# VectorE in place of GpSimd for the first FFN's first weight tiles, and group norm's reciprocal root by ScalarE and one Newton step

## The chip, the core and the metric

The kernel runs on one core of one Trainium2 chip. A core has five engines that run side by side, each with its own instruction queue, worked through in order: TensorE (PE; its weight loads are listed apart as PEld), VectorE (DVE), ScalarE (ACT), GpSimd (POOL) and SyncE (SP), which here issues the transfers. They synchronise by semaphores. The metric is the time of one execution on the device in microseconds; lower is better.

## The reference

Two layers over a sequence of 512 tokens of 1024 features, in float32. Layer 0 mixes tokens with RWKV-7 (a delta-rule recurrence over 16 heads of 64), layer 1 with a spatial gating unit (SGU). Each is followed by a SwiGLU FFN of width 2816; each sub-layer is wrapped in two RMS norms.

```python
def _rmsnorm(x, g):
    y = x32 * lax.rsqrt(jnp.mean(x32 * x32, axis=-1, keepdims=True) + RMS_EPS)
    return y * g

# end of _rwkv7_time_mix: group norm per head of 64, bonus, gate, output projection
    mu = jnp.mean(y, axis=-1, keepdims=True)
    var = jnp.mean(jnp.square(y - mu), axis=-1, keepdims=True)
    y = (y - mu) * lax.rsqrt(var + GN_EPS)
    y = y * gn_w.reshape(H, N) + gn_b.reshape(H, N)
    y = y + jnp.sum(r_h * k_h * r_k, axis=-1, keepdims=True) * v_h
    return (y.reshape(B, T, D) * g) @ w_o

def _swiglu(x, w_gate, w_up, w_down):
    return (jax.nn.silu(x @ w_gate) * (x @ w_up)) @ w_down

def reference(x, norm_gains, ...):
    for i in range(DEPTH):
        h = _rmsnorm(x, norm_gains[i, 0])
        h = _rwkv7_time_mix(h, ...) if i % 2 == 0 else _sgu_mixer(h, ...)
        x = x + _rmsnorm(h, norm_gains[i, 1])
        h = _swiglu(_rmsnorm(x, norm_gains[i, 2]), ...)
        x = x + _rmsnorm(h, norm_gains[i, 3])
    return x
```

## The kernel before

**Products in three parts.** To keep float32 precision, each large operand is split into a high part (rounded, `whi`, `hT` part 0) and a low part (the rest, `wlo`, `hT` part 1). A product is three matmuls: high by high, high by low, low by high (`mm3`, line 204). The split is two instructions: a copy to the rounded type on ScalarE (line 179) and a subtraction on VectorE (line 180). `weight` (line 182) loads a weight tile of 128x1024 elements into `wraw` by a transfer on SyncE's queue and splits it. With `pool=True` it has its own pair of lines: the copy on ScalarE (line 195) and the subtraction on GpSimd (line 196).

**RWKV (0 to about 450 us).** The heads go in four groups of four (b = 0 to 3). A written plan (`PLAN`) gives the order in which the program states the steps: projections (P), per-group features (E), matrices for chunks of 64 tokens (F, `front`), the triangular inverses (B, `back`: a recurrence of 15 steps on VectorE, lines 910 and 912, on a transposed matrix, then chains of small matmuls with copies into `bdT` between), the scan over chunks (S) and the finish (N). The finish of a group calls `group_norm`, `bonus` and `gated`. `group_norm` takes the mean over 64 (line 1038), subtracts it (1040), squares on ScalarE (1042), sums (1044), calls `rsqrt` on the 16 or 8 sums of each partition, and scales (1046). It runs for groups 0, 1 and 2 over all tokens and for group 3 in two halves of the tokens: five calls, whose roots begin at 287, 334, 396, 420 and 431 us. `gated` transposes on PE (`yt`, 1084), adds the bonus (1085), makes the gate by matmuls (1088) and multiplies (1089); `yt` and `gate` share one bank of PSUM.

**`rsqrt` (line 209).** A reciprocal root wholly on VectorE: scale and offset, a shifted integer guess in two steps, three Newton rounds of three steps: 12 instructions, each needing the one before it. The other routine, `rsqrt1` (line 248), used by the RMS norms, takes ScalarE's root (line 254), VectorE's reciprocal and one Newton step.

**The output projection (`out_proj`, line 273).** It works on two halves of 512 columns, each with four accumulators of 128 tokens. The last weight unit of each half is held back, and the accumulators are then closed token tile by token tile (tt = 0 to 3). `post0` squares half 0 (line 237 on ScalarE) and multiplies it by the gain (line 309 on VectorE), `post1` does the same for half 1 (lines 237 and 317), takes the root (`rsqrt1`) and adds to the residual stream (line 320). The tile `hn` of 1024 columns is scratch: `post1` writes its squares, which nobody reads, into columns 0 to 511 and the scaled half 1 into 512 to 1023. In the RWKV projection (the one called with `spare`), `post0` runs next to `post1` and writes its unread squares into columns 512 to 1023; after tile 0, line 312 computes a root whose result isn't used, so that ScalarE holds the table of the root function from there on. ScalarE has one set of function tables at a time and loads another by an instruction of its own (`ACT_TABLE_LOAD`); copies and squares run under each of the sets seen here. Before line 312 the set is that of the exponential. `norm.step` then transposes the rows of a finished token tile (line 267) and splits them into `hT` (line 60 on ScalarE, line 62 on VectorE).

**The first FFN's first pair.** `plain(0, None)` computes feature tiles j = 0 and 1, each from a gate and an up weight tile. These four tiles are the ones loaded with `pool=True`. Their matmuls go first over tokens 0 to 255, then over 256 to 511, so that they can begin while the last token tiles are still being normed. `Quads` adds up `hT` (line 105) for the later pairs, which use a scheme of seven block products (lines 387 and following). The second FFN receives its first four weight tiles from the SGU (`early`), without `pool`.

**What sets the order.** The program is stated in the order of the code, but the framework that builds it plans the order of each engine's instructions from its own estimates of their times (`schedule_with_timeline_sim=True`), within the data dependences, the banks and buffers, and the few places where the code pins an order. An edit to one instruction can therefore move others, also far behind it.

Of the kernel before, what the change touches and what calls it, by code (L numbers as in the profile page):

```python
# [13 lines left out]
P = 128  # L14
# [116 lines left out]
class Trunk:  # L131
# [77 lines left out]
    def rsqrt(self, ss, n, scale, eps):  # L209
# [13 lines left out]
            v.scalar_tensor_tensor(y, t, 1.5, y, op0=ALU.add, op1=ALU.mult)  # L223
        return y

    def bcast_row(self, row):

        t = self.gp.tile([P, D], F32, name="gain", tag="gain", bufs=2)
        self.nc.gpsimd.dma_start(out=t, in_=row.partition_broadcast(P))
        return t  # L230
# [42 lines left out]
    def out_proj(self, acts, wrows, nk, row, xts, store=None, tail=3, norm=None, spare=None, mid=None, after=()):  # L273


        nc = self.nc
        v = nc.vector
        gain = self.bcast_row(row)
        nu = nk // 2
        cols = [slice(0, 512), slice(512, 1024)]  # L280
        late = (1, 1) if spare else (0, tail)
        accs, f0, part = [None, None], [], []

        def mms(half, k, tt, w):
            tok = slice(tt * P, (tt + 1) * P)
            hi, lo = acts(k)
            self.mm3(accs[half][tt], (hi[:, tok], lo[:, tok]), w, k == 0, k == nk - 1)

        def unit(half, u):
            own = spare if half and u < nu - late[1] else None  # L290
            with ExitStack() as order:
                for ins in after:
                    order.enter_context(self.tc.issue_after(ins.ins))
                hi, lo = self.weight(wrows(u)[:, :, cols[half]], spare=own)
            return [(2 * u + j, (hi[:, j, :], lo[:, j, :])) for j in range(2)]

        def first(half):
            accs[half] = self.accs(half)
            for u in range(nu - late[half]):
                for k, w in unit(half, u):  # L300
                    for tt in range(TT):
                        mms(half, k, tt, w)

        def post0(tt, junk):
            acc = accs[0][tt]
            s = self.sumsq(acc, junk)
            if tt % 2 == 0:
                f0.append(self.f0p.tile([P, 2, 512], F32, name="f0", tag="f0", bufs=2))
            v.tensor_tensor(f0[-1][:, tt % 2, :], acc, gain[:, cols[0]], op=ALU.mult)
            part.append(self.part(s, 1.0 / D, RMS_EPS))  # L310
            if tt == (0 if spare else TT - 1):
                nc.scalar.activation(junk[:, 0:1], part[tt][0], AF.Sqrt)

        def post1(tt, hn):
            acc, lo, hi = accs[1][tt], hn[:, 0:512], hn[:, 512:1024]
            s = self.sumsq(acc, lo)
            v.tensor_tensor(hi, acc, gain[:, cols[1]], op=ALU.mult)
            y = self.rsqrt1(s, part[tt], 1.0 / D)
            for f, c in ((f0[tt // 2][:, tt % 2, :], cols[0]), (hi, cols[1])):
                v.scalar_tensor_tensor(xts[tt][:, c], f, y[:, 0:1], xts[tt][:, c], op0=ALU.mult, op1=ALU.add)  # L320
                if store is not None and tt == TT - 1:
                    nc.sync.dma_start(out=store[tt * P:(tt + 1) * P, c], in_=xts[tt][:, c])
            if store is not None and tt < TT - 1:
                nc.sync.dma_start(out=store[tt * P:(tt + 1) * P, :], in_=xts[tt])

        hn_tile = lambda: self.sm.tile([P, D], F32, name="hn", tag="hn", bufs=2)
        first(0)
        if not spare:
            for tt in range(TT):
                post0(tt, hn_tile()[:, 0:512])  # L330
        if mid:
            mid()
        first(1)
        ends = [[kw for u in range(nu - late[half], nu) for kw in unit(half, u)] for half in range(2)]
        for tt in range(TT):
            for half in range(2):
                for k, w in ends[half]:
                    mms(half, k, tt, w)
            if norm and tt >= LAG:
                norm.step(tt - LAG, xts[tt - LAG])  # L340
            hn = hn_tile()
            if spare:
                post0(tt, hn[:, 512:1024])
            post1(tt, hn)
        if norm:
            for tt in range(TT - LAG, TT):
                norm.step(tt, xts[tt])
            norm.finish()
# [5 lines left out]
    def ffn(self, li, xts, norm, store=None, nxt=None, early=()):  # L354
# [98 lines left out]
        def plain(n, yb):  # L453
            act = self.slot([P, 2, T], F32, "act")
            acts.append(act)
            for f in range(2):
                j = 2 * n + f
                ws = early.pop(0) if early else [self.weight(w[:, :, j * P:(j + 1) * P], pool=j < 2) for w in wgu]
                pp = [self.bank("gu", "gu") for _ in range(2)]
                for c in ((g, u) if j < 2 else (slice(0, 512),)):  # L460
                    for w, ps in zip(ws, pp):
                        for kt in range(KT):
                            self.mm3(ps[:, c], (w[0][:, kt, :], w[1][:, kt, :]), (hT[kt][:, 0, c], hT[kt][:, 1, c]),
                                     kt == 0, kt == KT - 1)
                yb = norm.row() if yb is None else yb
                t = act[:, f]
                v.tensor_tensor(t, pp[0], yb, op=ALU.mult)
                a.activation(t, t, AF.Silu)
                v.tensor_tensor(t, t, pp[1], op=ALU.mult)
                nc.gpsimd.tensor_tensor(t, t, yb, op=ALU.mult)  # L470
            return yb
# [58 lines left out]
    def rwkv(self, x0):  # L530
# [3 lines left out]
        with ExitStack() as ctx:  # L534
# [496 lines left out]
            def group_norm(Y, tts):  # L1031

                n, n4 = len(tts), 4 * len(tts)
                ts = slice(tts[0], tts[-1] + 1)
                y4 = Y[:, ts].rearrange("p t q (h v) -> p (t q h) v", h=2)
                yf = Y[:, ts].rearrange("p t q f -> p (t q f)")
                mu = self.sm.tile([P, n4], F32, name="mu", tag="mu", bufs=2)
                v.tensor_reduce(mu, y4, axis=mybir.AxisListType.X, op=ALU.add)
                v.tensor_scalar(mu, mu, 1.0 / 64, None, op0=ALU.mult)
                v.tensor_tensor(y4, y4, mu.unsqueeze(2).broadcast_to([P, n4, C]), op=ALU.subtract)  # L1040
                sq = self.sm.tile([P, n4, C], F32, name="hn", tag="hn", bufs=2)
                a.activation(sq.rearrange("p q v -> p (q v)"), yf, AF.Square)
                va = self.sm.tile([P, n4], F32, name="va", tag="va", bufs=2)
                v.tensor_reduce(va, sq, axis=mybir.AxisListType.X, op=ALU.add)
                rs = self.rsqrt(va, n4, 1.0 / 64, GN_EPS)
                v.tensor_tensor(y4, y4, rs.unsqueeze(2).broadcast_to([P, n4, C]), op=ALU.mult)

            def bonus(b, o):
# [244 lines left out]
```

## Time and profile before

| | |
|---|---|
| median of 3 runs | 1354.4 us (1348.42 to 1357.36) |
| the profiled execution: time, span | 1345.89 us, 1344.2 us |
| mean granted TensorE clock | 0.979 |
| busy: PE, VectorE, ScalarE, GpSimd | 1279.7, 898.5, 694.9, 166.3 us |
| the four GpSimd subtractions | 461.67, 465.19, 469.19 and 472.66 us, 2.35 to 2.71 us each |
| the unread root of line 312 | 446.64 us: 1.28 us table load, 0.20 us root |

A row of a timeline gives start, duration, engine, line, operation, output<-inputs, shapes and count, and in brackets how long the engine was idle before and what ended that. A row of a table of stretches gives the stretch, its length, the busy time of PE, PEld, DVE, ACT and POOL with instruction counts, then the granted clock of TensorE (1.00 is full speed), the transfer engines' share and GB/s. Idle time of an engine that nobody waits for costs nothing.

### The profile page before, as it was taken

The numbers are of one execution on the slowest core, as the hardware profiler recorded it, in microseconds if no ns is written. First come the engines' busy times: TensorE is split into PE (matmuls) and PEld (weight loads), VectorE is DVE, ScalarE is ACT, GpSimd is POOL, SyncE is SP. The second block draws the span as 40 slices with busy tenths as digits, with TensorE's granted clock in tenths as the row PEclk, the third lists the DMA queues.
The fourth block names the chain that finished last, engine by engine and source line by source line (L and its number), as shares of the span: only waits on it lengthen the run. The fifth ranks groups of instructions, "written<-read, shape, count | busy, mean of one in ns | idle before, by whom it ended". The sixth has DMA issues, their size and how long they took to land.

```text
span 1344.2 us, 24525 instructions
## 1 busy us (share of the span) xinstructions
PE 1279.7 (95%) x9812; PEld 1115.3 (83%) x9812; DVE 898.5 (67%) x1520; ACT 694.9 (52%) x1240; POOL 166.3 (12%) x306
## 2 busy tenths in 40 slices
PE   5999999988989799999999999999999999999997
PEld 3677799887767698899998887878888999998886
DVE  7975846667856589778775325575689878785223
ACT  7976884757443554445454314543464455464221
POOL 0000373665000121000000002020002000000000
PEclk9999999989889999999999999999999999999999
DMA  5146683412143233333323332343430443323231
GB/s 159 47 107 169 165 199 127 123 47 78 45 139 106 72 91 101 107 114 108 106 87 110 94 112 91 93 140 98 142 95 2 125 126 95 97 78 125 94 94 63
DMA packets 217266, 140.10 MB, mean 104 GB/s; under 512 B 67856, under 2 KB 193344, under 8 KB 217152
## 3 DMA queue, kind: packets, MB, share of 16 engines
q1 hardware_dynamic: 215856, 133.81, 34.6%
q0 software_dynamic: 1296, 4.72, 1.0%
q8 instruction: 77, 1.26, 0.4%
q14 instruction: 37, 0.30, 0.1%
HBM read 124.35 MB, written 14.16 MB: 103 GB/s over the span
## 4 chain that ended last, share of the span: by engine, by line
PE 58%; DVE 5%; ACT 1%; issue 1%; DMA 0%; SPq 0%; DVEq 0%; ACTq 0%
PE acc L204 24%; PE Q L204 11%; PE Z L204 7%; PE R L204 7%; PE gu L204 5%; PE u L204 3%; DVE wlo L180 1%; DVE wsum L387 1%; PE s L1227 1%; PE ptr L267 0%; ACT whi L179 0%; DVE braw L106 0%; DVE hT L62 0%; DVE bc L180 0%; DVE x L320 0%
## 5 line engine op out<-in xcount | busy, mean ns | idle before, releaser
L180 DVE TENSOR_TENSOR wlo<-wraw,whi 128x1024 fp32r<-128x1024 f32 x109 | 133.6, 1226 | 197.8 <-ACT whi L179 197.4
L179 ACT CAST whi<-wraw 128x1024 fp32r<-128x1024 f32 x109 | 114.2, 1048 | 224.1 <-PE acc L204 140.9
L204 PE MATMUL acc<-whi,actw 128*128 128x512 f32 x704 | 220.7, 394 | 0.0
L204 PE MATMUL Q<-bc,whi 128*128 128x256 f32 x864 | 157.2, 282 | 3.5 <-ACT hn L431 2.2
L204 PEld LDWEIGHTS acc<-whi,actw 128*128 128x128 f32 x704 | 132.3, 188 | 30.7
L204 PE MATMUL acc<-wlo,actw 128*128 128x512 f32 x352 | 138.7, 394 | 0.0
L204 PEld LDWEIGHTS Q<-bc,whi 128*128 128x128 f32 x864 | 133.8, 190 | 4.3 <-ACT hn L431 2.6
L179 ACT CAST whi<-wsum 128x1024 fp32r<-128x1024 f32 x72 | 75.2, 1050 | 90.3 <-PE Q L204 31.3
L204 PE MATMUL Q<-bc,wlo 128*128 128x256 f32 x432 | 121.7, 282 | 0.0
L204 PE MATMUL Z<-bc,whi 128*128 128x256 f32 x576 | 106.8, 283 | 0.0
L204 PE MATMUL R<-bc,whi 128*128 128x256 f32 x576 | 105.3, 281 | 0.8 <-ACT whi L179 0.8
L180 DVE TENSOR_TENSOR wlo<-wsum,whi 128x1024 fp32r<-128x1024 f32 x72 | 87.0, 1220 | 20.3 <-ACT whi L179 19.1
L204 PE MATMUL gu<-hT,whi 128*128 128x256 f32 (+1 forms) x384 | 91.5, 331 | 5.0 <-DVE hT L62 3.6
L179 ACT CAST whi<-wq 128x1024 fp32r<-128x1024 f32 x54 | 56.6, 1049 | 66.0 <-PE R L204 22.3
L204 PEld LDWEIGHTS R<-bc,whi 128*128 128x128 f32 x576 | 88.9, 188 | 1.3 <-ACT whi L179 1.0
L204 PEld LDWEIGHTS Z<-bc,whi 128*128 128x128 f32 x576 | 89.7, 190 | 0.1
L180 DVE TENSOR_TENSOR wlo<-wq,whi 128x1024 fp32r<-128x1024 f32 x54 | 67.4, 1250 | 28.8 <-ACT whi L179 28.7
L204 PE MATMUL Z<-bc,wlo 128*128 128x256 f32 x288 | 81.4, 283 | 2.3 <-DVE wlo L180 2.3
L204 PE MATMUL proj<-xsp,whi 128*128 128x512 f32 x256 | 82.4, 401 | 1.3 <-ACT r L674 1.3
L204 PEld LDWEIGHTS Q<-bc,wlo 128*128 128x128 f32 x432 | 82.1, 190 | 0.0
L204 PE MATMUL R<-bc,wlo 128*128 128x256 f32 x288 | 81.0, 281 | 0.0
L204 PEld LDWEIGHTS acc<-wlo,actw 128*128 128x128 f32 x352 | 66.0, 188 | 15.3
(346 smaller groups left out, 2841.2 us busy)
## 6 DMA issues: line engine op xcount, KB each, us to landing
wraw<-in_ffn_w_down_dram SPq DMA_DIRECT2D x44, 512.0 KB, 3.7
wq<-in_ffn_w_gate_dram SPq DMA_DIRECT2D x72, 256.0 KB
wq<-in_ffn_w_up_dram SPq DMA_DIRECT2D x72, 256.0 KB, 4.2
wraw<-in_rwkv_w_rkv_dram SPq DMA_DIRECT2D x24, 512.0 KB, 5.4
wraw<-in_sgu_w_in_dram SPq DMA_DIRECT2D x16, 512.0 KB, 4.5
x<-in_x_dram SPq DMA_DIRECT2D x8, 512.0 KB, 3.4
ST<-sb SPq DMA_DIRECT2D x8, 512.0 KB
MV<-sa SPq DMA_DIRECT2D x32, 128.0 KB, 3.5
```

Source lines behind the costliest of these rows:

```text
L179: self.nc.scalar.copy(hi, src)
L180: self.nc.vector.tensor_tensor(lo, src, hi.bitcast(F32), op=ALU.subtract)
L204: self.nc.tensor.matmul(out, l, r, start=start, stop=stop, skip_group_check=resumed)
L387: v.tensor_tensor(s, x, y, op=ALU.add)
L1227: mm(acc[:, tt * P:(tt + 1) * P], vt[tt][:, m * P:(m + 1) * P], wsT[:, m, :], start=True, stop=True)
```

## The change

Group norm's reciprocal root is computed by a new routine, `rsqrtn`: scale and offset on VectorE, the root on ScalarE, the reciprocal and one Newton step of three instructions on VectorE. The unread root at line 312 is left out where the projection is the RWKV one (it stays in the others). In that projection `post0` writes its unread squares into columns 0 to 511. The first FFN's first four weight tiles are split like all others, the subtraction on VectorE.

```diff
+    def rsqrtn(self, ss, n, scale, eps):
+        sm, v = self.sm, self.nc.vector
+        c, r, m = (sm.tile([P, n], F32, name=t, tag=t) for t in ("nr_a", "nr_y", "nr_t"))
+        v.tensor_scalar(c, ss, scale, eps, op0=ALU.mult, op1=ALU.add)
+        self.nc.scalar.activation(r, c, AF.Sqrt)
+        v.reciprocal(r, r)
+        v.tensor_tensor(m, r, r, op=ALU.mult)
+        v.scalar_tensor_tensor(m, m, -0.5, c, op0=ALU.mult, op1=ALU.mult)
+        v.scalar_tensor_tensor(r, m, 1.5, r, op0=ALU.add, op1=ALU.mult)
+        return r
...
             part.append(self.part(s, 1.0 / D, RMS_EPS))
-            if tt == (0 if spare else TT - 1):
+            if not spare and tt == TT - 1:
                 nc.scalar.activation(junk[:, 0:1], part[tt][0], AF.Sqrt)
...
             if spare:
-                post0(tt, hn[:, 512:1024])
+                post0(tt, hn[:, 0:512])
             post1(tt, hn)
...
-                ws = early.pop(0) if early else [self.weight(w[:, :, j * P:(j + 1) * P], pool=j < 2) for w in wgu]
+                ws = early.pop(0) if early else [self.weight(w[:, :, j * P:(j + 1) * P]) for w in wgu]
...
-                rs = self.rsqrt(va, n4, 1.0 / 64, GN_EPS)
+                rs = self.rsqrtn(va, n4, 1.0 / 64, GN_EPS)
```

## The prediction

> **What bounds the kernel now.** I read the page first, then the chain of waits, then tables of equal stretches, and last the timeline of each engine around the edited lines. The page:
>
> ```profile
> span 1344.2 us, 24525 instructions
> PE 1279.7 (95%) x9812; PEld 1115.3 (83%) x9812; DVE 898.5 (67%) x1520; ACT 694.9 (52%) x1240; POOL 166.3 (12%) x306
> PE 58%; DVE 5%; ACT 1%; issue 1%; DMA 0%; SPq 0%; DVEq 0%; ACTq 0%
> ```
>
> PE is busy for 95% of the span and heads the chain that ended last. Its own work is not edited, so a gain can come from two places only: the 64.5 us (1344.2 - 1279.7) in which PE waits, and stretches in which it runs at a reduced clock. The edits lie between the first group norm (287 us) and the first FFN pair (about 476 us). The table of stretches (columns: stretch, its length, busy time of PE, weight load, VectorE = DVE, ScalarE = ACT, GpSimd = POOL, then the granted clock, DMA share, GB/s) shows where PE loses there:
>
> ```profile
> 328.00:338.00 10.00, 6.91 (x190) 6.01 (x186) 9.83 (x31) 5.17 (x9) 3.69 (x8) 0.67 0.31 106
> 338.00:348.00 10.00, 7.93 (x89) 6.61 (x88) 9.47 (x25) 3.22 (x6) 0.00 (x0) 0.50 0.01 2
> 283.61:287.02 3.41, 1.53 (x14) 1.40 (x13) 3.33 (x4) 2.99 (x8) 2.24 (x5) 0.99 0.23 79
> 287.02:290.44 3.42, 3.42 (x17) 3.20 (x16) 3.01 (x14) 2.87 (x7) 1.76 (x4) 0.51 0.03 5
> 386.01:389.42 3.41, 1.95 (x13) 1.27 (x10) 1.43 (x3) 1.62 (x2) 0.00 (x0) 1.00 0.11 28
> 389.42:392.84 3.42, 2.67 (x23) 2.28 (x25) 2.62 (x4) 1.47 (x4) 0.00 (x0) 1.00 0.60 171
> 447.45:450.86 3.41, 1.25 (x8) 0.94 (x7) 2.11 (x8) 3.05 (x11) 0.00 (x0) 0.99 0.10 29
> 450.86:454.28 3.42, 3.42 (x11) 2.65 (x10) 3.04 (x11) 0.25 (x1) 0.00 (x0) 0.51 0.56 152
> 464.51:467.93 3.42, 0.80 (x5) 0.35 (x3) 3.35 (x7) 3.42 (x13) 2.35 (x1) 0.99 0.53 153
> 467.93:471.34 3.41, 1.36 (x6) 1.36 (x7) 3.41 (x12) 2.83 (x8) 2.15 (x1) 0.50 0.52 154
> ```
>
> I chose these 3.41 us stretches because the clock changes on that grid. After a stretch in which PE was busy for 1.25 or 1.53 us the next runs at about half clock; after one with 1.95 us it runs at full clock. So a wait costs its own length, and, where it takes PE below somewhere between 1.53 and 1.95 us of 3.41 (45% to 57%), up to 1.7 us more (3.42 x (1 - 0.51)).
>
> **Part A, the root in group norm (five calls).** The old routine issues 12 VectorE instructions a call, the new one 5 and a ScalarE root: 35 fewer on VectorE, 5 more on ScalarE. One of the root's groups by line from 276 to 460 us (busy us, mean ns), then VectorE's timeline in the first call, in the second, and after the third and the last:
>
> ```profile
> L222 DVE SCALAR_TENSOR_TENSOR nr_t<-nr_t,nr_a 128x16 f32<-128x16 f32 (+1 forms) x15 | 2.6, 176 | 0.3
> 283.63 1.22 DVE L1044 TENSOR_REDUCE va<-hn 128x16 f32<-128x1024 f32 x1 [2.48 <-ACT hn L1042]
> 287.25 0.38 DVE L214 TENSOR_SCALAR nr_a<-va 128x16 f32<-128x16 f32 x1
> 290.15 0.17 DVE L223 SCALAR_TENSOR_TENSOR nr_y<-nr_t,nr_y 128x16 f32<-128x16 f32 x1
> 335.75 0.28 DVE L912 TENSOR_TENSOR Dm<-Dm,tm 128x110 f32<-128x110 f32 x1
> 335.94 0.17 DVE L222 SCALAR_TENSOR_TENSOR nr_t<-nr_t,nr_a 128x16 f32<-128x16 f32 x1
> 336.06 0.28 DVE L910 TENSOR_TENSOR tm<-LX,Dm 128x120 f32<-128x120 f32 x1
> 342.13 0.28 DVE L912 TENSOR_TENSOR Dm<-Dm,tm 128x120 f32<-128x120 f32 x1
> 342.45 0.27 DVE L910 TENSOR_TENSOR tm<-LX,Dm 128x110 f32<-128x110 f32 x1
> 414.89 0.69 DVE L1089 TENSOR_TENSOR ob<-gate,ob 128x512 f32<-128x512 f32 x1 [5.66 <-PE gate L1088]
> 439.99 0.42 DVE L1089 TENSOR_TENSOR ob<-gate,ob 128x256 f32<-128x256 f32 x1 [3.30 <-PE gate L1088]
> ```
>
> 35 x 0.176 us is 6.2 us of VectorE time. Little of it is on PE's path. First call: PE is busy all through 287.02 to 290.44. Second call, where VectorE is full: the triangular recurrence (L910, L912) steps from 335.75 to 336.06 with a root step between, 0.31 us, and from 342.13 to 342.45 without one, 0.32 us, so the root steps fill gaps and their removal returns almost nothing. After the third and the last call VectorE stands idle for 5.66 and 3.30 us until PE has made the gate. If nevertheless all reached PE, the first call would give 7 of the 12 steps of its 3.07 us (290.32 - 287.25), less the trip to ScalarE of about 0.4: 1.4 us, and the second some 0.6, so -2.0 is the lower end.
>
> Against that stand a new wait and a table load. VectorE takes its instructions in order: its reciprocal waits for the root, and behind it wait the bdT copies, the recurrence and the MV sums, for which PE waits. The row at 283.63 shows the price of such a wait in this very routine: VectorE stood 2.48 us for ScalarE's square. The first root also needs its table (1.28 us) and itself (0.29; both rows stand in part B) on a ScalarE that is busy for 2.99 of 3.41 us there; its copies behind would be 1.6 us late. Upper end: 2.5 + 1.6 = +4.1. No row shows this root in this place; between the ends I take 0, nearest to the recurrence's rows, because the order of instructions is planned anew with the root in it and has other work to put between.
>
> The Trainium skill (ScalarE: Activation LUTs, "What ACT_TABLE_LOAD costs") charges about 1.38 us of drain beside the 1.28 us load, 2.66 us in all. The rows of part B have the next instruction directly behind the load. By the page, A's upper end would be +5.5, and B's removal below would be worth 1.38 us more.
>
> **Part B, the end of the output projection (L312, and the scratch half).** Since the group norm leaves the root's table loaded, the early root at L312 goes. ScalarE's timeline, VectorE's, PE's:
>
> ```profile
> 446.64 1.28 ACT L312 ACT_TABLE_LOAD   x1 [0.86 <-DVE rh L245]
> 447.93 0.20 ACT L312 ACTIVATE hn<-rc 128x1 f32<-128x1 f32 x1
> 448.04 0.58 ACT L237 ACTIVATE hn<-acc 128x512 f32<-128x512 f32 x1
> 449.18 0.29 ACT L254 ACTIVATE rr<-ss,rc 128x1 f32<-128x1 f32 x1
> 448.75 0.69 DVE L317 TENSOR_TENSOR hn<-acc,gain 128x512 f32<-128x512 f32 x1 [2.12 <-ACT hn L237]
> 450.26 0.40 DVE L1089 TENSOR_TENSOR ob<-gate,ob 128x256 f32<-128x256 f32 x1
> 448.27 0.28 PE L1088 MATMUL gate<-sgb,g2x 96*128 96x256 f32 x1
> 450.72 0.64 PE L1084 MATMUL yt<-ident,Y 128*128 128x128 f32 x2 [2.16 <-DVE ob L1089]
> ```
>
> This is a chain: load and root on ScalarE, then the square at 448.04, then L317, for which VectorE idled 2.12 us, then L1089, then PE's transpose after 2.16 us. The gate was done at 448.55, so L1089 could come 1.7 us earlier at most; the square can come 1.4 us earlier (448.04 - 446.64). I take 1.2. That lifts PE's busy time in 447.45:450.86 from 1.25 to about 2.4 of 3.41 us, above the 1.95 that kept full clock, so the next stretch gains up to 1.7 us; I take 1.5, for VectorE must keep up. B = -2.7, ends -3.1 and 0 (the next accumulator, not this load, may be what the square would wait for). Nothing is added here, so B has no end above 0. Moving the scratch to the other half costs nothing: L317 still waits for the square of the accumulator it reads. Once this stall is gone, the next late thing is the start of the FFN, part C.
>
> The Trainium skill (TensorE: Matmul & The Clock Gate, "HAM oscillation") asks only for no idle gap over about 3.4 us. The wait of 2.16 us in front of a half-clock stretch speaks against it; by the page the sum would lose the 1.5.
>
> **Part C, the four wlo tiles.** GpSimd's timeline, VectorE's, PE's, and the page's price of the same operation on VectorE:
>
> ```profile
> 465.19 2.35 POOL L196 TENSOR_TENSOR wlo<-wraw,whi 128x1024 fp32r<-128x1024 f32 x1 [1.13 <-ACT whi L195]
> 472.66 2.44 POOL L196 TENSOR_TENSOR wlo<-wraw,whi 128x1024 fp32r<-128x1024 f32 x1 [0.76 <-ACT whi L195]
> 463.06 0.69 DVE L309 TENSOR_TENSOR f<-acc,gain 128x512 f32<-128x512 f32 x1 [3.55 <-ACT hn L237]
> 465.54 2.02 DVE L257 SCALAR_TENSOR_TENSOR rt<-rr,rm 128x1 f32<-128x1 f32 x1
> 471.73 3.99 DVE L105 TENSOR_TENSOR braw<-hT 128x256 f32<-128x256 f32 x5
> 484.32 1.09 DVE L105 TENSOR_TENSOR braw<-hT 128x256 f32<-128x256 f32 x3
> 469.98 0.58 PE L204 MATMUL gu<-hT,whi 128*128 128x256 f32 x1 [3.29 <-DVE hT L62]
> ```
>
> A subtraction on VectorE takes 1.22 us, as the group has it:
>
> ```profile
> L180 DVE TENSOR_TENSOR wlo<-wraw,whi 128x1024 fp32r<-128x1024 f32 x109 | 133.6, 1226 | 197.8 <-ACT whi L179 197.4
> ```
>
> Added: 4 x 1.22 = 4.9 us on VectorE. Returned: the 128x1 step at 465.54 took 2.02 us and ended as GpSimd's tile did (467.54), against 0.17 for such small steps: 1.8; the five L105 at 471.73 took 0.80 each beside GpSimd, the three at 484.32 without it 0.36: 2.2. Net +0.9. The first tile fits into the 3.55 us idle before 463.06. On the path to hT, whose late half PE awaited for 3.29 us, 1.8 goes and one tile (1.2) may come: -0.6. The third and fourth tiles lie before the hT of the last tokens: 2.4 - 2.2 = +0.2. C = -0.4. Clock: both stretches from 464.51 to 471.34 lie far below the threshold (0.80, 1.36) and 0.6 us more won't lift the first; I take 0. Ends: -3.5 (1.8 and a half-clock stretch of 1.7) and +3.2 (two tiles ahead of hT, 2.4 - 1.8 = 0.6, 0.9 later, and a stretch of 1.7).
>
> **Sum.** 0 - 2.7 - 0.4 = -3.1 us. The profiled execution took 1345.9 us (its span of 1344.2 and 1.7 around it), so it becomes 1342.8. The three runs before have a median of 1354.4, 8.5 above the profiled one; against them the forecast is 1351.3, given as 1351.
>
> **Rivals** (times against the median).
> 1. All of it counts: A -2.0, B -3.1, C -3.5: -8.6, 1346. For it: VectorE is full from 328 to 348 us, where PE has its longest half-clock stretch. Against: the recurrence's unchanged step.
> 2. Slower: VectorE stands at the reciprocal, in its first call and again in the second. It decides once the root comes later than the 1.4 us that the missing steps save. Price: 4.1 + 1.7 for a half-clock stretch, then 2.5 + 1.7: +10.0; with B and C +6.9: 1361. For it: the 2.48 us at 283.63. Against: the planned order has other work for the gap.
> 3. VectorE becomes the bound at the FFN's start: C +3.2 eats B: +0.5, 1355. For it: VectorE busy 3.35 and 3.41 of 3.41 us.
> 4. No clock comes back, since another wait takes the place of the one in B within the same stretch: -1.6, 1353. It is also what the Trainium skill's clock rule (TensorE: Matmul & The Clock Gate, "HAM oscillation") would give.
> 5. The new plan shuffles the work from 287 us on with results that no row prices: up to 15 either way.
>
> **Numbers.** Chances: forecast 0.35; rivals 0.22, 0.13, 0.11, 0.11, 0.08. Runs of the same kernel differ by 9 us (1348.4 to 1357.4), so about 1%, 13.5 us, is what can be told from no change. Each case carries about 4.5 us to either side for that. Forecast and rivals 1, 3 and 4 span 1341 to 1360; with rival 2 mostly below that end, 1340 to 1360 leaves out less than 2 in 10. Faster by over 1% (under 1341) takes the low tail of rival 1 and half of rival 5: 0.12. Slower by over 1% (over 1368) takes the tails of rivals 2 and 5: 0.05. Within 1%: 0.83.
>
> **What would show it.** A: 25 VectorE steps under the new routine, a table load in front of the first root and none in the projection; wrong if VectorE's idle time before the reciprocal exceeds 1.4 us with PE waiting then. B: no load at 446 us, PE's wait for L1089 at about 1 us, no half-clock stretch behind it. C: no small VectorE step of 2 us; PE's wait for hT under 3 us. The prediction is wrong if PE's waits before 287 us or after 490 us change, or if PE's summed waits move by over 6 us.

## The result and the profile after

The changed kernel took 1338.3 us (median of 4 runs, 1334.5 to 1340.7) against 1351.4 for the kernel before in the same series (4 runs): a ratio of 0.990 with a 95% interval of 0.987 to 0.993. Another series gave 1338.0 against 1349.4, 0.992 (0.990 to 0.994). The forecast was 1351, a gain of 3.1, with a range of 1340 to 1360; the gain is 11 to 13 us, and the time lies 2 us below the range.

Lines of the kernel after that lie behind line 225 stand 12 higher than before (L949, the copies into `bdT`, is L961; L910 and L912, the recurrence, are L922 and L924). From the page of the kernel after:

```profile
span 1339.0 us, 24501 instructions
...
PE 1278.9 (96%) x9812; PEld 1114.0 (83%) x9812; DVE 892.5 (67%) x1489; ACT 694.8 (52%) x1244; POOL 160.7 (12%) x302
```

PE waits for 60.1 us of the span (1339.0 - 1278.9), 4.4 less than before. The two profiled spans differ by 5.2 us only: the profiled run of before lies 5.5 us under the median of its series (1345.9 against 1351.4), that of after 2.5 above its own (1340.7 against 1338.3), which together makes the 13.1 us between the medians.

**Where the time went.** I took the same events in both traces and compared the distance between them. The largest change lies around group norm's second call. VectorE's timeline, first before, then after, at the two ends of that stretch:

```profile
266.97 1.99 DVE L916 STREAM_TRANSPOSE Dt<-Dm 128x1024 f32<-128x1024 f32 x1
367.27 0.68 DVE L935 TENSOR_TENSOR Qs<-Qp,id 128x512 f32<-128x512 f32 x1
```

```profile
270.62 1.95 DVE L928 STREAM_TRANSPOSE Dt<-Dm 128x1024 f32<-128x1024 f32 x1
363.24 0.68 DVE L947 TENSOR_TENSOR Qs<-Qp,id 128x512 f32<-128x512 f32 x1
```

The stretch took 100.3 us before and 92.6 after: -7.7. As rows of a table of stretches, before and after:

```profile
266.97:367.27 100.30, 88.78 (x1615) 76.59 (x1615) 73.91 (x174) 57.87 (x138) 39.98 (x92) 0.88 0.19 54
```

```profile
270.62:363.24 92.62, 83.71 (x1615) 72.39 (x1615) 70.98 (x160) 59.34 (x141) 39.85 (x92) 0.94 0.22 59
```

PE's idle time fell from 11.5 us (100.30 - 88.78) to 8.9, and the same 1615 matmuls kept it busy for 5.1 us less, at a mean clock of 0.94 in place of 0.88. So about two thirds of the gain is busy time that went by at a higher clock. What differs in the stretch is the planned order, and in it first of all where the copies into `bdT` of the group before stand in VectorE's queue. Before and after, in the order of time, with the last and first steps around them:

```profile
327.40 1.97 DVE L896 STREAM_TRANSPOSE LX<-LA 128x1024 f32<-128x1024 f32 x1
...
336.26 0.17 DVE L223 SCALAR_TENSOR_TENSOR nr_y<-nr_t,nr_y 128x16 f32<-128x16 f32 x1
336.35 0.67 DVE L949 COPY bdT<-Tp 32x512 f32<-32x512 f32 x1
...
337.97 0.69 DVE L949 COPY bdT<-Tp 32x512 f32<-32x512 f32 x1
...
343.92 0.69 DVE L968 COPY bdT<-T2p 32x512 f32<-32x512 f32 x1
```

```profile
328.18 1.95 DVE L908 STREAM_TRANSPOSE LX<-LA 128x1024 f32<-128x1024 f32 x1 [0.53 <-POOL LA L845]
330.05 0.64 DVE L961 COPY bdT<-Tp 32x512 f32<-32x512 f32 x1
...
332.29 0.69 DVE L961 COPY bdT<-Tp 32x512 f32<-32x512 f32 x1
...
338.94 0.24 DVE L232 RECIPROCAL nr_y<-nr_y 128x16 f32<-128x16 f32 x1
...
341.44 0.69 DVE L980 COPY bdT<-T2p 32x512 f32<-32x512 f32 x1
```

Before, the first copy started 8.95 us after the start of the `LX` transpose, behind group norm's mean, square sum and the first Newton round. After, it starts 1.87 us after it, ahead of all of them. PE needs these copies for its next products (`mp`). PE's waits from 318 to 368 us, before and after (line that waited, who released it, us in total, times, longest):

```profile
PE mvt L923 <- ACT MVt L926: 3.1, 1, 3.1
PE mp L973 <- DVE bdT L968: 1.9, 1, 1.9
```

```profile
PE Q2p L967 <- issue: 0.8, 1, 0.8
PE Yp L1034 <- ACT su L1026: 0.8, 1, 0.8
```

The waits of 3.1 and 1.9 us are gone. They hang on two queues. The one of 1.9 us is for a `bdT` copy on VectorE, the one of 3.1 us for a copy into `MVt` on ScalarE. ScalarE's timeline, before and after:

```profile
331.36 1.06 ACT L1042 ACTIVATE hn<-Y 128x1024 f32<-128x1024 f32 x1 [1.84 <-issue]
332.44 1.07 ACT L926 COPY MVt<-mvt 128x512 f32<-128x512 f32 x2
```

```profile
335.02 1.06 ACT L1054 ACTIVATE hn<-Y 128x1024 f32<-128x1024 f32 x1
```

Before, ScalarE idled 1.84 us in front of group norm's square, with the `MVt` copies behind it. The square reads what VectorE's subtraction of the mean (L1040) writes, which was done at 331.01 us; the profile names no engine for this wait, so its cause is read from the order and the code. After, the mean and the subtraction stand behind the first `bdT` copy, and ScalarE has other copies to do until the square can start: it doesn't idle there.

The two stretches quoted in the prediction, 328 to 338 and 338 to 348 us, read so after (columns as there):

```profile
328.00:338.00 10.00, 7.86 (x205) 6.32 (x204) 9.63 (x17) 7.84 (x18) 5.85 (x13) 0.91 0.39 122
338.00:348.00 10.00, 9.71 (x84) 8.81 (x82) 9.56 (x32) 3.64 (x6) 0.00 (x0) 0.75 0.01 2
```

PE went from 6.91 and 7.93 us busy at clock 0.67 and 0.50 to 7.86 and 9.71 at 0.91 and 0.75. VectorE is as full as before. So it isn't VectorE's load that has changed, but the order in which it and ScalarE work.

**The other steps in the trace after.** The first call on ScalarE and VectorE; the projection end on ScalarE and PE, with its stretches; the FFN's start on VectorE and PE:

```profile
288.79 1.28 ACT L231 ACT_TABLE_LOAD   x1
291.04 0.22 ACT L231 ACTIVATE nr_y<-nr_a 128x16 f32<-128x16 f32 x1 [0.97 <-DVE nr_a L230]
...
445.45 0.29 ACT L266 ACTIVATE rr<-ss,rc 128x1 f32<-128x1 f32 x1
445.63 0.59 ACT L249 ACTIVATE hn<-acc 128x512 f32<-128x512 f32 x1
```

```profile
291.29 0.25 DVE L232 RECIPROCAL nr_y<-nr_y 128x16 f32<-128x16 f32 x1 [0.28 <-ACT nr_y L231]
...
461.00 1.21 DVE L180 TENSOR_TENSOR wlo<-wraw,whi 128x1024 fp32r<-128x1024 f32 x1
```

```profile
445.49 0.44 PE L1096 MATMUL yt<-ident,Y 128*128 128x128 f32 x2 [0.79 <-DVE ob L1101]
446.66 0.50 PE L204 MATMUL acc<-whi,oT 128*128 128x512 f32 x1 [0.73 <-ACT oT L179]
...
463.85 0.58 PE L204 MATMUL gu<-hT,whi 128*128 128x256 f32 x1 [1.13 <-DVE hT L62]
```

```profile
445.33:448.75 3.42, 2.52 (x13) 2.02 (x14) 3.25 (x13) 1.57 (x7) 0.00 (x0) 1.00 0.51 153
448.75:452.16 3.41, 3.41 (x16) 2.62 (x15) 3.33 (x9) 0.41 (x1) 0.00 (x0) 1.00 0.02 7
```

The table load lies in front of the first root and none in the projection. VectorE stood 0.28 us at the reciprocal. PE's wait for the gate's product at the projection end fell from 2.16 to 0.79 us (with 0.73 behind it), and the stretches from there on run at full clock in this trace.

### The profile page after: what moved, and what is told of

Same layout as the page of the kernel before. It is cut to its first block, busy times and chain, and to the rows that moved or that the text cites. A ratio compares the mean times of both kernels' runs of the same rounds, so it can differ in the third digit from the quotient of the medians.

```text
span 1339.0 us, 24501 instructions
## 1 busy us (share of the span) xinstructions
PE 1278.9 (96%) x9812; PEld 1114.0 (83%) x9812; DVE 892.5 (67%) x1489; ACT 694.8 (52%) x1244; POOL 160.7 (12%) x302
## 4 chain that ended last, share of the span: by engine, by line
PE 62%; DVE 10%; DMA 3%; ACT 2%; issue 2%; SPq 1%; POOL 1%; DVEq 0%; ACTq 0%; POOLq 0%
PE acc L204 27%; PE Q L204 10%; PE Z L204 7%; PE R L204 7%; PE gu L204 5%; PE u L204 3%; DVE wlo L180 2%; DMA wq<-in_ffn_w_up_dram 1%; DVE wsum L399 1%; PE gh L992 1%; DMA wraw<-in_rwkv_w_o_dram 1%; DVE hT L62 1%; PE s L1239 1%; ACT whi L179 0%; DVE bc L180 0%
## 5 line engine op out<-in xcount | busy, mean ns | idle before, releaser
L180 DVE TENSOR_TENSOR wlo<-wraw,whi 128x1024 fp32r<-128x1024 f32 x113 | 139.6, 1235 | 194.3 <-ACT whi L179 193.7
L179 ACT CAST whi<-wraw 128x1024 fp32r<-128x1024 f32 x113 | 118.4, 1049 | 232.0 <-PE acc L204 146.0
```

Source lines behind the costliest of these rows:

```text
L179: self.nc.scalar.copy(hi, src)
L180: self.nc.vector.tensor_tensor(lo, src, hi.bitcast(F32), op=ALU.subtract)
```

## The experiments

Parts as in the prediction: A is the root in group norm, B the projection end (early root and scratch half), C the four `wlo` tiles. At first there were two theories of A's gain. *Order*: the planned order of the second call, with `bdT` early, makes it. *Steps*: the fewer VectorE steps make it.

### Each part alone

A alone puts `rsqrtn` into the kernel before; B alone has the two edits of the projection; C alone has the edit of the weight tiles.

> Part A alone on the kernel before: the new root in group norm; the early root at the projection, its scratch half and the GpSimd tiles stay. Three theories. Steps: the 35 missing VectorE instructions (6.2 us) count, -5 to -7 us. Order: the new root matters because the plan of the stretch from 326 to 350 us comes out with the bdT copies ahead of group norm's mean, where before they stood behind it and PE waited 3.1 and 1.9 us and ran at half clock; -6 to -8 us, all of it won between 325 and 350 us, about +1.6 lost at the first call to the table load. The prediction's: steps hidden, 0, at most -1.3 because the load at the projection is gone too.

> Part B alone: the early root at the projection is left out and the scratch half moved, old root, GpSimd tiles. The load of the root's table is then still needed for the projection's first real root. All theories: the square comes 1.4 us earlier but the load now stands before the first root, behind which no PE work waits at once: -1 to 0 us; the half-clock stretch behind 450 us may go (-1.7 more). If B itself is worth the 2.7 us of the prediction without A, PE's wait for L1101 (L1089 before) falls from 2.2 to about 1 us.

> Part C alone: the four subtractions on VectorE, all else as before. The prediction's: -0.4 us (-3.5 to +3.2), no 128x1 step of 2 us on VectorE, PE's wait for hT 3.3 -> 2.7. Order theory: about -2.5, since from 400 to 575 us the changed kernel won 5.1 us of which B is 2.7. If C is worth nothing, the drift against before stays at 0 through 575 us.

Measured beside 1351.2 us for the kernel before: A 1345.3, ratio 0.9957 (0.9938 to 0.9975); B 1350.7, 0.9998 (0.9976 to 1.0019); C 1348.3, 0.9978 (0.9956 to 1.0001). A gains 5.9 us, all others little: most of the gain was not where the forecast had it. A's time lies in the range of both theories, so it doesn't tell them apart. B alone can't save the load. ScalarE's and PE's timeline of B alone:

```profile
460.94 1.28 ACT L266 ACT_TABLE_LOAD   x1
```

```profile
463.10 0.44 PE L1096 MATMUL yt<-ident,Y 128*128 128x128 f32 x2 [1.90 <-DVE ob L1101]
```

Without A, the load only moves to the projection's first used root, and PE still waits 1.90 us. B alone also leaves the order of all instructions as it was.

### More or fewer steps, and an order forced by hand

Group norm keeps the old root, with one, two or four Newton rounds in place of three:

```diff
-                rs = self.rsqrt(va, n4, 1.0 / 64, GN_EPS)
+                rs = self.rsqrt(va, n4, 1.0 / 64, GN_EPS, 1)    # 2, 4
```

> The kernel before with one Newton round instead of three in group norm's root: 6 VectorE steps a call, no ScalarE root, no table load (the root is accurate to some 0.2% only, two rounds of its refinement are left out). Steps theory: 6 steps x 5 calls x 0.17 = -5.2 us. Order theory: the planned order from 326 us has the bdT copies right behind the transpose, as in the changed kernel, so -5 to -8, between 325 and 350 us. If the ScalarE root itself brought the gain: 0.

> The kernel before with two Newton rounds instead of three: 9 steps a call (one round of refinement left out). Steps theory: -2.6 us. Order theory: the bdT copies stand in the middle, behind the mean and half of the recurrence but ahead of the root: between 0 and -4, not in proportion to the steps.

> The kernel before with four Newton rounds instead of three: 15 steps a call. Steps theory: +2.6 us. Order theory: the bdT copies stand behind the root as before, so 0 to +1.5; the order after that stretch differs, which can be worth some us either way.

Two kernels keep the old root and pin the order of the second call: one holds the mean behind the first `bdT` copy, the other holds the mean and four recurrence steps each behind one of the copies.

```diff
-                v.tensor_reduce(mu, y4, axis=mybir.AxisListType.X, op=ALU.add)
+                with tc.issue_after(late.ins) if late else ExitStack(): v.tensor_reduce(mu, y4, axis=mybir.AxisListType.X, op=ALU.add)
```

> The kernel before, old 12-step root and all, with one more order: the mean of the second group norm call (from 326 us) may not be issued on VectorE before the first bdT copy of group 2's inverse. Only that stretch's order changes. Order theory: most of part A's gain comes without any step saved, -4 to -8 us between 325 and 350 us, and PE's wait for MVt of 3.1 us is gone. Steps theory and the prediction's: 0 within 2 us.

> The kernel before, old 12-step root, with the order of the stretch from 326 us forced: on VectorE the first bdT copy of group 2 goes ahead of the mean of group 1's norm and of step 0 of group 3's recurrence, the second ahead of step 1, the Q2 copy ahead of step 3, the copy from T2p ahead of step 6 (the first attempt held back only the mean, and the plan put the copies behind the recurrence). Order theory: no step is saved, yet -4 to -8 us appear between 325 and 350 us, and PE's waits for MVt (3.1) and for the bdT copy from T2p (1.9) shrink. Steps theory and the prediction's: 0 in that stretch; behind it the plan may differ.

Measured: one round 1348.4, 0.9977 (0.9958 to 0.9997); two rounds 1364.4, 1.0084 (1.0054 to 1.0114); four rounds 1361.6, 1.0074 (1.0047 to 1.010); the mean held 1353.6, 1.0007 (0.998 to 1.003); all held 1360.6, 1.0068 (1.004 to 1.010). The steps theory falls: with two rounds VectorE has 15 steps fewer than before and the kernel is 12 us slower. The times that the order theory gave were missed as well: it had -5 to -8, 0 to -4 and 0 to +1.5 us for one, two and four rounds, and the runs gave -4.0, +12.0 and +9.3. In the stretch itself it came closer (-7.0, -1.5 and +2.3 in the table of all runs below); the rest is what the plan changed further on.

The two pinned kernels missed too: neither gained. With the mean held, the plan moved the copies still further back, behind 11 of the 15 steps of the recurrence. PE's wait for `MVt` shrank from 3.1 to 0.3 us, as expected, but its wait for `bdT` grew from 1.9 to 4.3: the two waits do hang on two queues. With all held, the copies are early in the queue, but VectorE stands in front of the first until PE has made what it copies; that copy, the stretch and the waits of that kernel:

```profile
334.32 0.68 DVE L961 COPY bdT<-Tp 32x512 f32<-32x512 f32 x1 [4.18 <-PE Tp L956]
```

```profile
328.00:338.00 10.00, 7.84 (x278) 6.51 (x278) 4.88 (x7) 6.15 (x15) 4.76 (x13) 0.91 0.40 122
```

```profile
PE mp L985 <- DVE bdT L980: 2.2, 1, 2.2
PE us L1021 <- DVE MV L994: 2.1, 1, 2.1
```

VectorE is busy for 4.88 us of 10 where it had 9.83. So an early place in the queue alone is not shown to gain anything. What gains is the whole order that the plan makes when it puts the copies early of itself.

### Order and steps taken apart

Which root the *first* call has decides the planned order of the *second*: in the kernels built here the copies come early with 5 or 6 VectorE steps in the first call's root, in the middle with 9, and late with 12 or 15. So the whole change was split by call: once the second call alone keeps the old root (its 12 steps, but `bdT` early), once the first call alone does (the second call has the 5 steps, but `bdT` late).

```diff
-                rs = self.rsqrtn(va, n4, 1.0 / 64, GN_EPS)
+                rs = (self.rsqrtn if self.__dict__.setdefault('gnc', []).append(1) or len(self.gnc) in (1, 3, 4, 5) else self.rsqrt)(va, n4, 1.0 / 64, GN_EPS)    # mirror: (2, 3, 4, 5)
```

> The changed kernel once more, beside the next three, so that they can be compared with it on one chip. Both theories: 1338 us, between 1334 and 1341, ratio 0.990 to the kernel before.

> The whole change, but the second group norm call (the one beside the recurrence) keeps the old root with its 12 VectorE steps. The plan still puts the bdT copies right behind the LX transpose: that order is set by the first call's root. Order theory (the gain of part A comes from the place of the bdT copies): as the changed kernel, 1338 to 1342 us; in the stretch from 346 to 367 us it still gains 7 us or more on the kernel before; the seven more steps cost 7 x 0.176 = 1.2 us at the most. Steps theory (fewer VectorE steps in the stretch where VectorE is full): most of part A's 5.9 us is gone, 1344 us or more.

> The mirror of the run before: the whole change, but the first group norm call keeps the old root; the second and the later ones have the new one. The plan now puts the bdT copies of the second call late, behind the whole new root. Order theory: part A's gain is gone, 1343 to 1349 us, with PE's waits for the bdT copies or MVt of 3 us or more between 318 and 368 us and no gain over the kernel before between 346 and 367 us. Steps theory: the second call has its five steps, so the gain stays: 1337 to 1341 us.

> Parts A and B without C (the four wlo tiles stay on GpSimd). Alone, A measured 1345.3 (-5.9 us), B 1350.7 (-0.5), C 1348.3 (-2.9): together -9.3, while the whole change gave -13.1. If B is worth its 2.7 us only where A leaves the table loaded, ab gives -5.9 - 2.7 = -8.6, about 1342.7 us, and C adds its 2.9 and a little more. If instead the surplus comes from C beside A, ab is at 1345 (as A alone).

Measured beside 1349.4: the changed kernel 1338.0; old root in the second call 1341.6, 0.9938 (0.992 to 0.996); old root in the first call 1359.8, 1.0081 (1.005 to 1.011); A and B without C 1337.8, 0.9907 (0.989 to 0.993). The old steps with the early order keep 7.8 of the 11.4 us, the new steps with the late order lose everything and 10 us more. The first is inside the range of the order theory. The mirror is slower than either theory had it, and A and B are faster than both forecasts for them. VectorE's timeline of the mirror, and PE's, here and further on in the projection:

```profile
327.96 1.96 DVE L908 STREAM_TRANSPOSE LX<-LA 128x1024 f32<-128x1024 f32 x1
335.79 0.25 DVE L232 RECIPROCAL nr_y<-nr_y 128x16 f32<-128x16 f32 x1
337.05 0.67 DVE L961 COPY bdT<-Tp 32x512 f32<-32x512 f32 x1
```

```profile
PE mvt L935 <- ACT MVt L938: 3.1, 1, 3.1
```

```profile
433.59 0.66 PE L1071 MATMUL vt<-ident,hn 128*128 128x128 f32 x4 [1.29 <-ACT ob L1073]
435.03 0.69 PE L1096 MATMUL yt<-ident,Y 128*128 128x128 f32 x2 [0.78 <-ACT ob L1073]
```

The wait of 3.1 us is that of the kernel before. The second place, at 433 us, is one reason why the mirror is slower than before, not just equal (+9.2 us in the second stretch of the table below; a weight sum in the second layer comes with 6.3 more in the third). Its plan puts PE's transposes `vt` of the last group's bonus behind the projection's first products, PE waits 1.29 and 0.78 us, and clock 0.50 follows from 435 to 440 us.

### What B adds beside A

A, B and C alone add up to -9.3; A and B together gave -11.6. Yet the trace of A alone has no load at the projection end, and PE's wait there is 0.79 us already. These runs were made side by side: A alone; A without the early root; A and B; and the whole change with the new root in the first call only.

```diff
-            if tt == (0 if spare else TT - 1):          # A without the early root: this edit alone
+            if not spare and tt == TT - 1:
```

> Part A alone once more, beside the next three. Its trace has no table load at the projection end (the group norm leaves the table in place) and PE's wait for L1101 there is 0.8 us, not 2.16. Theory of order: most of the whole gain is here, -8 to -10 us, about 1341 us; the -5.9 of the first call was low by the spread of the two calls (each ratio carries +-0.002, 2.7 us). Theory of an own gain of B: -5 to -6 us again, about 1345 us.

> Part A and the early root of the projection removed; the scratch half as before. Theory of order: within 1 us of part A alone (the root that goes is 0.2 us without a load). Theory that the early root matters: as A with both edits.

> Parts A and B, without C, once more: 1338 us. Theory of order: within 3 us of part A alone. Theory that the scratch half is what gains (the second half's product no longer waits for the square that writes the same half): 4 to 6 us below part A and below A with the early root removed.

> The whole change, with the new root in the first group norm call only; the four later calls keep the old root and its 12 VectorE steps. The plan puts the bdT copies of the second call early, as in the changed kernel. Theory of order: 1339 to 1343 us, as the run with the old root in the second call alone (1341.6). If the new root itself is worth its steps in the later calls: 1346 us or more.

Measured beside 1350.1: A 1343.6, 0.9950 (0.993 to 0.997); A without the early root 1343.9, 0.9942 (0.992 to 0.996); A and B 1336.2, 0.9879 (0.985 to 0.991); new root in the first call only 1340.0, 0.9914 (0.988 to 0.994). The early root brings nothing that shows (0.3 us); the scratch half, which was thought to cost and bring nothing, comes with some 7 us. The first call's root alone brings nearly the whole gain of the change. Its own steps can't be what brings it: that root took 3.07 us before and takes 1.42 in the trace after (290.85 to 292.27 us). The 7 us are not at the projection (second stretch of the table below). PE's timeline, then VectorE's, of A alone, in the second layer, 600 us behind the edit:

```profile
1043.11 0.58 PE L204 MATMUL Z<-bc,whi 128*128 128x256 f32 x1 [2.98 <-DVE bc L180]
```

```profile
1039.56 1.23 DVE L399 TENSOR_TENSOR wsum<-wq 128x1024 f32<-128x1024 f32 x1 [2.63 <-DMA wq<-in_ffn_w_up_dram]
1040.70 1.22 DVE L399 TENSOR_TENSOR wsum<-wsum,wq 128x1024 f32<-128x1024 f32 x1
1041.84 1.22 DVE L180 TENSOR_TENSOR bc<-tsum,bc 128x1024 fp32r<-128x1024 f32 x1
```

The same place of A and B, VectorE:

```profile
1038.39 1.22 DVE L399 TENSOR_TENSOR wsum<-wsum,wq 128x1024 f32<-128x1024 f32 x1
1039.53 1.22 DVE L180 TENSOR_TENSOR bc<-tsum,bc 128x1024 fp32r<-128x1024 f32 x1
1040.66 2.35 DVE L399 TENSOR_TENSOR wsum<-wq 128x1024 f32<-128x1024 f32 x2
```

In A alone the plan put one weight sum, `wsum<-wq`, ahead of `bc`, and VectorE stood 2.63 us for its transfer with `bc` behind it. PE waited 2.98 us, and its clock was 0.66 on average from 1040 to 1050 us. In A and B that sum stands behind `bc`, and PE doesn't wait.

Two more runs have the scratch half without that order (A and the half, early root kept; two sums ahead of `bc`) and that order without the half (A and C):

> Part A and the scratch half; the early root of the projection stays. In its plan the second layer's bc (L180, at about 1040 us) stands behind two sums (L399) that wait for their DMA, one more than in A alone. Theory of the plan: PE waits 3 us or more for bc there and the run is as slow as A alone or slower, 1343 to 1348 us, although it has the scratch half. Theory that the half as such gains: 1336 to 1339 us, as A with both of B's edits.

> Parts A and C without B (scratch half and early root as before). In its plan the second layer's bc stands ahead of both sums, as in the changed kernel. Theory of the plan: no wait for bc, 1336 to 1341 us, as the changed kernel, without any of B's edits. Theory that the half as such gains: 1343 to 1345 us, as A alone.

Measured beside 1350.9: A and the half 1344.4, 0.9938 (0.991 to 0.996); A and C 1342.9, 0.9943 (0.992 to 0.996). The first has the time that the theory of the plan gave, with the half and as slow as A alone, but not the wait: PE doesn't stand for `bc`. It waits 4.7 us for `hT` at the start of the first FFN and 2.5 us at 1060.7 us for a `wlo`, ahead of which VectorE stood 3.03 us for the transfer of two more sums. The second missed: PE has no wait for `bc`, but the run is no faster than A alone. It loses at the start of the first FFN, where PE waits 1.69 and 1.20 us. So the place of `bc` is not all that B brings beside A; the plan of the first FFN is a further part. From the fourth `x<-hn,ry,x` of line 332 to the third `wsum<-wsum,wq` (478.3 to 543.9 us before) A and C took 2.6 us more than the kernel before, the change 1.2 and 1.4 less (two traces): some 4 us lie there.

### All runs together

The distance between the same events in each trace, less that of the kernel before. *First*: from the second `Dt` transpose to the fourth `Qs` sum, the stretch of 100.3 us above. *Second*: from the mean of the fifth group norm call to the second `x<-hn,ry,x` of line 332 (426.0 to 455.7 before, 29.7 us). *Third*: from the tenth such step to the 36th `wsum<-wsum,wq` (976.1 to 1196.5 before, 220.4 us).

| kernel | ratio | `bdT` copies | sums ahead of `bc` | first | second | third |
|---|---|---|---|---|---|---|
| after | 0.990 | early | 0 | -7.7 | -0.2 | +1.8 |
| after, again | 0.992 | early | 0 | -8.3 | -0.2 | +1.8 |
| A and B | 0.991 | early | 0 | -9.5 | -0.2 | +1.6 |
| A and B, again | 0.988 | early | 0 | -8.3 | +0.7 | +1.4 |
| new root in call 1 only | 0.991 | early | 0 | -6.5 | +5.0 | +1.0 |
| old root in call 2 only | 0.994 | early | 0 | -7.7 | +2.7 | +2.2 |
| A and C | 0.994 | early | 0 | -8.4 | -0.7 | +1.5 |
| one Newton round | 0.998 | early | 0 | -7.0 | +4.9 | +2.1 |
| A | 0.996 | early | 1 | -7.2 | -0.7 | +7.2 |
| A, again | 0.995 | early | 1 | -7.5 | -0.7 | +5.0 |
| A without the early root | 0.994 | early | 1 | -8.7 | -0.6 | +6.4 |
| A and the half | 0.994 | early | 2 | -7.5 | +0.1 | +5.3 |
| C | 0.998 | late | 0 | +0.9 | 0.0 | +0.7 |
| B (order of before) | 1.000 | late | 0 | +7.7 | -0.5 | +1.9 |
| mean held | 1.001 | later | 0 | +5.2 | -0.4 | +0.1 |
| all held | 1.007 | early, forced | 0 | +4.4 | +0.8 | +0.8 |
| old root in call 1 only | 1.008 | late | 1 | +0.7 | +9.2 | +6.3 |
| four Newton rounds | 1.007 | late | 1 | +2.3 | +4.9 | +4.7 |
| two Newton rounds | 1.008 | in the middle | 2 | -1.5 | +10.1 | +8.5 |

Each is one profiled run, and B, whose order is that of before, is off by 7.7 us in the first stretch (clock 0.66 from 340 to 350 us), so a single figure there says little. The groups say more: every kernel whose plan puts the copies early of itself gains 6.5 to 9.5 us in the first stretch, no other over 1.5; and every kernel with a sum ahead of `bc` loses 4.7 to 8.5 in the third, no other over 2.2. In the 12 kernels of the first group PE idles for 7.2 to 9.7 us of the first stretch and has 6.8 to 17.1 us at half clock; in the other seven and in the kernel before it is 10.5 to 14.6 and 13.7 to 34.1.

## Why the prediction was wrong

**The bound** was read right: PE, its waits and its clock, between 287 and 490 us. The largest loss was even quoted, the stretches at 328 and 338 us. It was not asked what PE waited for there (`MVt` 3.1 us, `bdT` 1.9 us) and what stood in VectorE's and ScalarE's queues ahead of that; only the price of the root's own steps was. The rule for the clock, half after 1.53 us busy and full after 1.95, doesn't hold even in the trace it was read from: PE was busy for 2.09 us from 273.32 to 276.73 and for 2.07 from 327.93 to 331.34, and half clock followed both.

**Part A**: the step that failed is "between the ends I take 0 ... because the order of instructions is planned anew with the root in it and has other work to put between". That the root's steps fill gaps agrees with the runs: with the new root in the first call only (28 VectorE steps more than the change) the kernel is at 0.991, as the change. The new wait stayed small too: 0.28 us in the first call, against a limit of 1.4, so rival 2 doesn't occur there. (No row showed the trip of about 0.4 us to ScalarE in the lower end; these 0.28 us are what VectorE stood for it.) But a new plan was taken as something that cushions, not as something that shifts. A alone measured -5.9 and -6.5 us, outside its lower end of -2.0. In its two traces the first stretch is 7.2 and 7.5 us shorter: the new order around the second call took away PE's waits of 3.1 and 1.9 us and part of the half-clock time, and for that no term of the sum stood. The same plan put a weight sum ahead of `bc` in the second layer, and the third stretch lost 7.2 and 5.0 us, against 1.0 to 2.2 in the early kernels without one. Whether A would be faster by the difference isn't shown, for A and C, which has no such sum, isn't.

**Part B**: most of the mechanism was right: no load, and the wait down from 2.16 to 0.79 us (about 1 was forecast). The 1.5 us for the clock were not secured: the same waits of 0.79 and 0.73 us were followed by full clock in the trace after and by half clock in that of A and B, again (last section). Two more things were wrong. It comes with A, as A alone has it; and its -2.7 was too large: from the mean of the fifth call to the copy `hn<-yb` at 492.0 us A alone, A again and A without the early root took 65.0, 64.5 and 64.4 us, 66.0 before, so 1.0 to 1.6 less, and PE's own progress (the 100th matmul `gu<-hT,whi`, also 66.0 before) was 66.3, 65.8 and 65.8, almost as before. "Moving the scratch to the other half costs nothing" holds of the instruction (B alone: 0.9998), not of the plan: beside A and without the early root it came with 7 us, in part through the place of `bc`.

**Part C**: as told, no 2 us step of one column, and PE's waits for `hT` in front of the FFN's products fell from 1.4 and 3.3 us to 0.9 and 1.4, though its transposes now wait 1.7 us for `hT`, which they did not before. The 0.80 us of each of the five L105 steps was the mean of a merged row: one took 2.60 us, the others 0.41, so GpSimd's tile held up one step. The 2.2 us come out the same, and in C alone all 12 such steps take 0.40 to 0.42. -0.4 was forecast; alone it gave -2.9 (-5.9 to +0.1), beside A and B nothing (1338.0 with it, 1337.8 without). The size is inside the ends given, and stays unclear.

**The rivals.** Rival 5, "the new plan shuffles the work from 287 us on with results that no row prices: up to 15 either way", is what happened, in both directions: from 0.988 to 1.008 among kernels whose own instructions differ by a few us. It had a chance of 0.08, and a gain of over 1% one of 0.12. Rival 1 (-8.6) came nearest in size, for other reasons. Of the signs named against the prediction, the one that came true is that PE's waits behind 490 us change: not in the kernel after, but in A alone.

What stays open: why the framework's plan puts the copies early when the first call is short (shown is only that it does), and why the second stretch takes 5 us more in the run with the new root in call 1 and in the one with one round (PE waits 2.5 and 2.6 us there for the cast `oT`, and in the first of them that cast stood 1.83 us for its transfer). Of B's 7 us beside A, 3.4 to 5.8 lie in the third stretch; the first FFN, from 455.7 to 543.9 us, has 2 at most (A and B 1.9 and 0.6 us less than before; the three traces of A within 0.6 of it). The rest is not assigned.

## What to carry to other kernels

Where the framework orders the instructions from its own estimates, an edit of a microsecond has two effects: its own price, and the plan's answer to it, which can be ten times as large, of either sign, and hundreds of microseconds away. So compare the planned order of each engine before and after the edit, look for steps that have moved past a copy or a product for which the bounding engine waits, and for steps that wait for a transfer and have moved ahead of one; price those first. And an edit that gains in this way hasn't shown that its idea was good: split it by part and by place, and see whether the gain goes with the idea or with the order.

## What the runs showed of the hardware

- The spread of a kernel's runs goes with the granted clock. In 99 runs of the kernel before, the span was 1356.4 us at a mean clock of 0.971 (median of 2), 1348.4 at 0.978 (24) and 1343.6 at 0.985 (1): about 1 us for 0.001. The six runs of the second series of the change have 0.981 to 0.986 and 1339.8 to 1335.0 us. At an equal clock the change is still 6 to 10 us ahead: 1346.1 (9 runs) against 1339.8 at 0.981, 1345.8 (5 runs) against 1336.0 and 1336.7 at 0.982. The rest goes with a higher clock.
- Where a stretch of the clock's grid begins can decide whether a wait costs clock. The clock changes on a grid of 3.41 us, and in the trace after the end of one such stretch (445.33 us) fell between the beginnings of PE's two waits at the projection end: 2.78 and 2.52 us busy, and full clock. In the trace of A and B, again, the same two waits fell into one stretch, and half clock followed:

```profile
442.70:446.11 3.41, 1.89 (x11) 1.31 (x10) 3.25 (x12) 2.74 (x11) 0.00 (x0) 1.00 0.15 35
446.11:449.52 3.41, 3.41 (x12) 2.83 (x11) 2.21 (x9) 0.41 (x1) 0.00 (x0) 0.50 0.34 126
```

  In the second trace of the change they fell into one stretch too, with 1.90 us busy (from 442.27 us), and full clock followed. At this place the bound thus lies near 1.9 us.
- The bound isn't the same elsewhere, so busy time alone doesn't decide. In the trace of before, 2.09 and 2.07 us were followed by half clock (from 273.32 and 327.93 us), and in the first trace of the change 2.42 us (from 278.08); in the second, 1.53 us (from 285.25) was followed by full clock. What else decides isn't shown.
